# Block order made at eviction, and a new table of delays for the order of TensorE's work, in a two-layer hybrid trunk step

## The chip, the core and the metric

The kernel runs on one core of a Trainium2 chip. The core has TensorE (PE: matmuls, with its weight loads shown as PEld), VectorE (DVE), ScalarE (ACT), GpSimd (POOL) and SyncE (SP, which here only issues DMAs). Each engine executes its own instructions in the order in which they stand in the program, and waits on semaphores where it needs another engine's or a DMA's result. The metric is the device time of one execution in microseconds (us), lower is better.

## The reference, cut to what matters

```python
def mixer_inputs(x, cond, norm_g, w_ada, b_ada, w_in):
    mod = jax.nn.silu(cond) @ w_ada + b_ada
    shift, scale, gate = jnp.split(mod, 3, axis=-1)
    h = rms_norm(x, norm_g) * (1 + scale) + shift
    return jnp.split(h @ w_in, IN_OFFSETS, axis=-1), gate
...
# per layer, on 1024 latent tokens (a grid of 16 rows x 64 columns) and 256 context tokens:
qa = rope_2d(rms_norm(aq, a_qn))                 # branch A: windowed attention
ya = window_attention(qa, ka, va, ka_c, va_c, a_sink) * jax.nn.silu(ag)
qb = rms_norm(bq, b_qn)                          # branch B: 2-D neighbourhood attention
yb = neighbourhood_attention(qb, kb, vb, kb_c, vb_c, b_rpb) * jax.nn.silu(bg)
xc = depthwise_conv(cx, conv_w, conv_b)          # branch C: gated linear recurrence (LRU)
a, u = rglru_coeffs(xc, wa, ba, wx, bx, lam)
yc = (hf + hb) * jax.nn.silu(cg)
z = sigmoid(ga)*(ya @ w_br[0]) + sigmoid(gb)*(yb @ w_br[1]) + sigmoid(gc)*(yc @ w_br[2])
x = x + gate * (z @ w_out)
```

Context tokens go through the same weights. Two layers are computed (`DEPTH` = 2).

## The kernel before, in words

**Numbers and jobs.** Activations lie in SBUF with channels on the 128 partitions and tokens along the free dimension. Every fp32 operand of a large product is split in two parts, a rounded one (`_h`, made by ACT) and the remainder (`_l`, made by DVE or POOL), and a product of one 128-row piece is three matmuls: h·h, h·l, l·h. A *job* (`job`) computes 128 output columns of a projection for three chunks of tokens, `CHUNKS`: two of 512 latent tokens and one of 256 context tokens. One latent chunk of an input projection is 8 pieces x 3 = 24 matmuls with 512 moving columns. Jobs are named by what they make: `k`, `q`, `v` (attention inputs), `gt` (merge gates), `sg` (the SiLU gates of the branches), `cx` (input of the recurrence), `br` (branch outputs), `po` (output projection).

**Raster and block order.** Branch B's attention works on blocks of 16 grid rows x 8 grid columns = 128 tokens, while tokens lie in raster order (64 columns per row). Before the change the jobs of branch B (k, q, v and sg of branch B, `perm`) read the moving operand already permuted, from `Hidden.cols`: the access pattern `"p (r a c) -> p a r c"` takes runs of 8 neighbouring columns, then jumps 64. What they write is then in block order.

**The order on TensorE.** Its order is fixed by hand: a planner (`Weave`) runs while the program is built. It keeps a planned clock `W.now`, which each `mm` and `transpose` advances by a fixed cost. Chains (the recurrence `lru`, the attention `chain`, the conditioning `ada_chain`) give way with a planned time at which they may go on, and until then the planner puts pieces of jobs on TensorE: first those in `W.need`, then those in `W.spare`. The delays come from the table `T`, in planned ns: `cv` (convolution of the recurrence to its first gate product), `kc` (load of cached keys to their transposes), `ac` (conditioning product to its transposition), `nx` (last output job to the norm of the next layer), `tb` (transposed probabilities to the values product), `soft`, `pace` and others for the attention. The order on the other engines and on SP's queue is left to the framework's scheduler, so it shifts with the planned order.

**Stages.** Per layer: the recurrence with `gt` jobs between its parts (`lg` are its gate products; `xc` the convolved input, split in `xh` and `xl`; `lR`, `lS`, `lJ` its elementwise tiles); then attention, B's four head pairs first, then A's, with projections and gates between (`sc`, `sl` scores, `pt` transposed probabilities, `PT` their two parts, `o` values product, `rt` row scales); then the merge, whose last addition into `acc` stands on POOL at L1196; then the output projection and the norm for the next layer (`nps`).

## Time and profile before

| | |
|---|---|
| time, median of 3 runs (lowest to highest) | 3274.76 us (3273.53 to 3278.29) |
| the profiled execution's own time | 3279.48 us |
| its span, first to last instruction | 3277.7 us |
| busy TensorE / VectorE / ScalarE / GpSimd | 96% / 54% / 51% / 30% |
| mean granted clock of TensorE | 0.986 of full |
| DMA queue of SP, share of the 16 DMA engines | 42.9% |

The busy time of TensorE is not its work at full speed: matmuls overlap in its pipeline, and a matmul that runs at half clock is busy for longer. So its speed is read from the distance between the starts of neighbouring matmuls, and its losses from stretches in which it stands idle or has a low granted clock. A time of a run and the span of the profile differ by what lies before the first and behind the last instruction.

### The profile page before, as it was taken

Reading aid. Unit: us, or ns where it says so; the run is one execution under the profiler, and the core shown is the slowest. Engines: PE = TensorE matmul, PEld = TensorE weight load, DVE = VectorE, ACT = ScalarE, POOL = GpSimd, SP = SyncE. Lnnn points to the kernel's source line nnn. Section 1 sums busy time; section 2 is a strip of 40 time slices with the busy share of each in tenths; the row PEclk is TensorE's granted clock in tenths of the full one; section 3 lists DMA queues with packets and bytes.
Section 4 is the critical chain, followed back from the end, with each engine's and each line's share of the span. In section 5 each row is a group of like instructions: output and inputs, shape, how many; then the busy total and the mean of one; then the engine's idle time right before and its main releaser. Section 6 shows DMA issues by size and latency. Waiting matters only on the chain.

```text
span 3277.7 us, 47968 instructions
## 1 busy us (share of the span) xinstructions
PE 3149.0 (96%) x17419; PEld 2652.8 (81%) x17419; DVE 1761.3 (54%) x3255; ACT 1679.3 (51%) x3570; POOL 973.8 (30%) x827
## 2 busy tenths in 40 slices
PE   8888899999999999999999899999999999999999
PEld 5666788888888888888778787888888888888887
DVE  5564346665765664444463443566656666645531
ACT  5556345555555655433245563555555555544422
POOL 3544322222420221236433233122222221112643
PEclk9999999999999999999999999999999999999999
DMA  8556455445542332654442326354455332337543
GB/s 281 145 136 137 124 154 144 113 141 154 154 127 73 99 94 71 215 187 138 128 126 90 71 62 165 107 153 136 121 152 158 100 100 80 90 102 244 186 145 103
DMA packets 414121, 435.02 MB, mean 133 GB/s; under 512 B 43872, under 2 KB 329148, under 8 KB 412604
## 3 DMA queue, kind: packets, MB, share of 16 engines
q1 hardware_dynamic: 407900, 414.91, 42.9%
q0 software_dynamic: 5664, 16.83, 1.7%
q8 instruction: 137, 2.24, 0.3%
q14 instruction: 100, 0.82, 0.1%
q10 hardware_dynamic: 320, 0.21, 0.0%
HBM read 298.12 MB, written 137.29 MB: 133 GB/s over the span
## 4 chain that ended last, share of the span: by engine, by line
PE 73%; DVE 10%; DMA 5%; ACT 5%; issue 3%; POOL 3%; SPq 1%; ACTq 0%; DVEq 0%; POOLq 0%
PE gt L217 14%; PE sg L217 10%; PE o L217 6%; PE br L217 6%; PE pt L224 5%; PE q L217 5%; PE po L217 5%; PE v L217 4%; PE k L217 4%; PE sc L217 3%; PE sl L217 3%; POOL acc L1196 1%; PE cx L217 1%; DMA out_dram<-lR 1%; DVE lR L684 1%
## 5 line engine op out<-in xcount | busy, mean ns | idle before, releaser
L426 ACT CAST PT<-pt 128x512 fp32r<-128x512 f32 (+2 forms) x528 | 269.6, 536 | 338.6 <-PE pt L224 336.2
L427 DVE TENSOR_TENSOR PT<-pt,PT 128x512 fp32r<-128x512 f32 (+2 forms) x528 | 319.8, 621 | 93.7 <-ACT PT L426 92.5
L950 DVE TENSOR_REDUCE st<-sc 128x1 f32<-128x512 f32 x256 | 176.3, 689 | 287.9 <-PE sc L217 287.3
L217 PE MATMUL gt<-hhl,wgt_h 128*128 128x512 f32 x736 | 302.1, 410 | 2.2 <-ACT wgt_h L421 2.2
L217 PE MATMUL gt<-hhl,wgt_l 128*128 128x512 f32 x736 | 292.7, 398 | 6.6 <-POOL wgt_l L422 6.6
L217 PE MATMUL gt<-hll,wgt_h 128*128 128x512 f32 x736 | 291.4, 396 | 0.0
L422 POOL TENSOR_TENSOR wgt_l<-wgt_r,wgt_h 128x512 fp32r<-128x512 f32 x110 | 165.7, 1512 | 352.0 <-ACT wgt_h L421 325.9
L224 PE MATMUL pt<-cst,P 128*128 128x128 f32 x1856 | 269.8, 273 | 0.1
L217 PE MATMUL po<-z,wpo_h 128*128 128x512 f32 (+1 forms) x768 | 210.3, 362 | 10.7 <-ACT z L426 9.3
L224 PEld LDWEIGHTS pt<-cst,P 128*128 128x128 f32 x1856 | 217.3, 141 | 3.7 <-PE pt L224 0.5
L217 PE MATMUL br<-yl,wbr_h 128*128 128x512 f32 (+1 forms) x576 | 204.5, 355 | 3.6 <-DVE yl L427 3.6
L967 ACT ACTIVATE P<-sc,st 128x512 f32<-128x512 f32 x256 | 175.1, 684 | 59.4 <-DVE st L961 58.9
L217 PE MATMUL br<-yh,wbr_h 128*128 128x512 f32 (+1 forms) x576 | 203.7, 354 | 1.1 <-DVE gl L1195 0.8
L217 PE MATMUL br<-yh,wbr_l 128*128 128x512 f32 (+1 forms) x576 | 204.2, 355 | 0.0
L217 PE MATMUL sc<-Kpast,Q 128*128 128x512 f32 x512 | 169.7, 413 | 14.0 <-ACT P L967 14.0
L422 POOL TENSOR_TENSOR wsg_l<-wsg_r,wsg_h 128x512 fp32r<-128x512 f32 x48 | 65.7, 1378 | 380.0 <-ACT wsg_h L421 369.2
L217 PE MATMUL o<-PT,Vpast 128*128 128x256 f32 x1024 | 177.2, 295 | 0.0
L969 ACT ACTIVATE P<-sl,st 128x384 f32<-128x384 f32 (+1 forms) x320 | 170.5, 533 | 5.0 <-DVE st L957 4.8
L217 PEld LDWEIGHTS gt<-hhl,wgt_l 128*128 128x128 f32 x736 | 140.5, 191 | 39.7 <-POOL wgt_l L422 7.9
L217 PEld LDWEIGHTS po<-z,wpo_h 128*128 128x128 f32 x768 | 137.6, 193 | 33.2 <-ACT z L426 10.2
L217 PEld LDWEIGHTS gt<-hhl,wgt_h 128*128 128x128 f32 x736 | 140.8, 191 | 26.7 <-ACT wgt_h L421 2.6
L217 PE MATMUL sg<-hhl,wsg_h 128*128 128x512 f32 x384 | 161.4, 420 | 0.0
(343 smaller groups left out, 8567.8 us busy)
## 6 DMA issues: line engine op xcount, KB each, us to landing
Q<-q_d SPq DMA_DIRECT2D x160, 256.0 KB
gl<-g_d SPq DMA_DIRECT2D x48, 640.0 KB
wgt_r<-in_w_in_dram SPq DMA_DIRECT2D x110, 256.0 KB
g_d<-tgt SPq DMA_DIRECT2D x92, 256.0 KB
wa<-in_w_ada_dram POOLq DMA_DIRECT2D x64, 256.0 KB, 4.3
q_d<-q_st SPq DMA_DIRECT2D x64, 256.0 KB
wpo_r<-in_w_out_dram SPq DMA_DIRECT2D x64, 256.0 KB
yg<-y_d SPq DMA_DIRECT2D x24, 640.0 KB
```

What stands on the lines that cost most here:

```text
L217: nc.tensor.matmul(out, a, b, start=start, stop=stop)
L224: nc.tensor.transpose(out, x, idn)
L422: nc.gpsimd.tensor_sub(lo, r, f32(hi))
L426: nc.scalar.copy(hi, x)
L427: nc.vector.tensor_sub(lo, x, f32(hi))
L684: nc.vector.tensor_tensor_scan(h, a, u, st if c0 < NLAT else 0.0, ALU.mult, ALU.add)
L950: nc.vector.tensor_reduce(cm, psc, AX.X, ALU.min)
L967: nc.scalar.activation(pt[:, nl * P:(nl + 4) * P], psc, AF.Exp, bias=m, scale=-1.0, accum_out=sums[:, t, x, 1:2])
L969: nc.scalar.activation(pt[:, :nl * P], loc, AF.Exp, bias=m, scale=-1.0, accum_out=sums[:, t, x, 0:1])
L1196: nc.gpsimd.tensor_add(z, z, g)
```

## The change

All projections now read raster order. Where branch B needs block order, the operation that takes the result out of PSUM reads it with the block pattern (`blocked`) and writes it in order. A chunk of 512 tokens is 8 grid rows, so it holds half of every block; keys stay in this half-block order and the score matmul reads two runs of 64 columns per block; queries and values are put in place by their DMAs to DRAM, which become two for each one. A first group of branch B now waits for both latent chunks of its queries. The SiLU gate of branch B is in raster order and is multiplied through a pattern; its factor 0.5 moves into the row scales. The last two additions of the merge in each layer move from POOL to DVE. The planner's cost of an fp32r matmul of 512 columns goes from 216 to 228 planned ns, and nearly all delays of `T` grow, some a little (`tb` 2000 to 2200), four of them much (`cv` 9500 to 16000, `kc` 3000 to 7000, `ac` 3500 to 7000, `nx` 3500 to 8000).

```diff
-T = dict(f1=9, f2=2, kc=3000, c0=10000, cq=1, gx=3, nx=3500, yo=1500, yi=1000, aq=9000, ac=3500, ms=1800, v=3000, tok=8260, scale=1000, t0=3100, tb=2000, o=2000, soft=7000, pace=9000, lg=300, lr=8000, cv=9500, le=4000)
+T = dict(f1=9, f2=2, kc=7000, c0=10000, cq=1, gx=3, nx=8000, yo=1500, yi=1000, aq=9000, ac=7000, ms=2000, v=3200, tok=8600, scale=1100, t0=3400, tb=2200, o=2200, soft=7600, pace=9400, lg=320, lr=8500, cv=16000, le=4200)
...
-        W.now += max(n, 256) / 2.4 * (4 if a.dtype == F32 else 1) + 3
+        W.now += n / 0.6 + 3 if a.dtype == F32 else max(n * 17 / 38.4, 109) + 1
...
+    def blocked(t):
+        return t.rearrange("p (r a c) -> p a r c", r=8, a=8)
+
+    def in_blocks(t):
+        return t.rearrange("p (a r c) -> p a r c", a=8, r=8)
...
-        def cols(self, ci, perm=False):
-            c0, N = CHUNKS[ci]
-            if not perm or c0 >= NLAT:
-                return [self.at(k, ci) for k in range(KD)]
-            a0 = c0 // P
-
-            def v(t):
-                return t.rearrange("p (r a c) -> p a r c", r=ROWS, a=8)[:, a0:a0 + 4]
-            return [(v(a), v(b)) for a, b in self.lat]
+        def cols(self, ci):
+            return [self.at(k, ci) for k in range(KD)]
...
-            nc.scalar.activation(sq[:, :N], ps, AF.Square)
-            nc.vector.tensor_scalar(raw[:, :N], ps, gain, None, ALU.mult)
+            src, to = (blocked(ps), in_blocks) if blocks else (ps, lambda t: t)
+            nc.scalar.activation(to(sq[:, :N]), src, AF.Square)
+            nc.vector.tensor_scalar(to(raw[:, :N]), src, gain, None, ALU.mult)
...
-                nc.scalar.copy(vr[:, :N], ps)
+                lat = perm and c0 < NLAT
+                nc.scalar.copy(in_blocks(vr) if lat else vr[:, :N], blocked(ps) if lat else ps)
...
-                    dma(v_d[l][br][p][:, c0 // P:c0 // P + nb], f32(st[:, :nb]))
+                    if lat:
+
+                        for h in range(2):
+                            dma(v_d[l][br][p][ci * HD:(ci + 1) * HD, h:8:2], f32(st[h * HD:(h + 1) * HD]))
...
                 def put(h, part):
-                    dma(q_d[l][br][p][:, h, :, c0:c0 + N], part)
+                    if perm and c0 < NLAT:
+                        for i in range(2):
+                            dma(q_d[l][br][p][:, h, i, 0:NLAT].rearrange("d (a i k) -> d a i k", i=2, k=HD)[:, :, ci],
+                                part[:, i].rearrange("d (a k) -> d a k", k=HD))
...
             def staged(g):
+                if g.br and not g.prompt:
+                    return W.when(("Q", 1, l, g.p, 0), ("Q", 1, l, g.p, 1))
...
+                elif br:
+                    kl = g.keys.K["lat"][:, kv].rearrange("p (i a k) -> p a i k", i=2, a=8)[:, kb[0]:kb[0] + nl]
...
-                nc.vector.tensor_copy(rb, tot.unsqueeze(2).to_broadcast([P, 4, HD]))
+                nc.vector.tensor_scalar(rb, tot.unsqueeze(2).to_broadcast([P, 4, HD]), 0.5 if br else 1.0, None, ALU.mult)
...
-                nc.vector.scalar_tensor_tensor(y, y, 0.5, g, ALU.mult, ALU.mult)
+                if b == 1:
+
+                    nc.vector.tensor_tensor(in_cols(y), in_cols(y), of_rows(g), ALU.mult)
+                    nc.vector.tensor_tensor(y[:, NLAT:], y[:, NLAT:], g[:, NLAT:], ALU.mult)
+                else:
+                    nc.vector.scalar_tensor_tensor(y, y, 0.5, g, ALU.mult, ALU.mult)
...
-                    nc.gpsimd.tensor_add(z, z, g)
+                    (nc.vector if b == 0 and k >= KD - 2 else nc.gpsimd).tensor_add(z, z, g)
```

How the new table moves instructions is seen at three places.

The first is VectorE in the recurrence of the second layer, between feature block 1 and block 2. `lS`, `lR` (the scans) and the addition at the end belong to block 1; `xc` and `xl` are the convolution that block 2's first gate products need. Before:

```order
L678 TENSOR_TENSOR lS_1_1_17485<-lS_1_1_17485,lJ_1_1_17425 128x1280
L684 SCALAR_TENSOR_TENSOR lR_1_1_17423<-lA_1_1_17483,colT_1471,lS_1_1_17485 128x1024
L684 SCALAR_TENSOR_TENSOR lR_1_1_17423<-lA_1_1_17483,lS_1_1_17485 128x256
L687 TENSOR_TENSOR lR_1_0_17422<-lR_1_0_17422,lR_1_1_17423 128x1280
L614 TENSOR_SCALAR xc_2_17743<-cx_2_17632,colT_1471 128x1283
L616 SCALAR_TENSOR_TENSOR xc_2_17743<-cx_2_17632,colT_1471,xc_2_17743 128x1283 x3
```

After:

```order
L614 TENSOR_SCALAR xc_2_17771<-cx_2_17630,colT_1469 128x1283
L684 SCALAR_TENSOR_TENSOR lR_1_0_17502<-lA_1_0_17561,colT_1469,lS_1_0_17563 128x1024
L616 SCALAR_TENSOR_TENSOR xc_2_17771<-cx_2_17630,colT_1469,xc_2_17771 128x1283
L684 SCALAR_TENSOR_TENSOR lR_1_0_17502<-lA_1_0_17561,lS_1_0_17563 128x256
L616 SCALAR_TENSOR_TENSOR xc_2_17771<-cx_2_17630,colT_1469,xc_2_17771 128x1283
L678 TENSOR_TENSOR lS_1_1_17569<-lS_1_1_17569,lJ_1_1_17505 128x1280
L616 SCALAR_TENSOR_TENSOR xc_2_17771<-cx_2_17630,colT_1469,xc_2_17771 128x1283
L684 SCALAR_TENSOR_TENSOR lR_1_1_17503<-lA_1_1_17567,colT_1469,lS_1_1_17569 128x1024
L684 SCALAR_TENSOR_TENSOR lR_1_1_17503<-lA_1_1_17567,lS_1_1_17569 128x256
L427 TENSOR_TENSOR xl_2_17777<-xc_2_17771,xh_2_17776 128x1283
L687 TENSOR_TENSOR lR_1_0_17502<-lR_1_0_17502,lR_1_1_17503 128x1280
```

The convolution stood behind the scans and behind the addition of L687; it now stands between the scans, and the addition behind all of it.

The second is SP's queue at the same place. `out_dram<-lR` stores one column of a scan's result, `y_d<-lR` the sum of L687, and `wl` are the weights of block 2's gates. Before:

```order
L686 DMA out_dram<-lR_1_0_17422 128x1
L686 DMA out_dram<-lR_1_1_17423 128x1
L688 DMA y_d_2_1_109<-lR_1_0_17422 128x1280
L605 DMA wl_2_17733<-in_lru_wa_dram 64x2x64 x2
L605 DMA wl_2_17733<-in_lru_wx_dram 64x2x64 x2
L413 DMA wcx_3_r_17899<-in_w_in_dram 128x4x128
```

After:

```order
L605 DMA wl_2_17761<-in_lru_wa_dram 64x2x64 x2
L605 DMA wl_2_17761<-in_lru_wx_dram 64x2x64 x2
L413 DMA wcx_3_r_17876<-in_w_in_dram 128x4x128
L686 DMA out_dram<-lR_1_0_17502 128x1
L698 DMA g_d_0_7_143<-tgt_0_70_0_17817 128x512
L413 DMA wcx_3_r_17882<-in_w_in_dram 128x4x128
L686 DMA out_dram<-lR_1_1_17503 128x1
```

The weight loads stood behind the stores of the block before them and now stand ahead of these.

The third is TensorE at the end of the second layer's attention, in the last group of branch A (`3_6`). Before:

```order
L224 MATMUL pt_3_6_0_3_28661<-cst,P_3_6_0_28398 128x128
L224 MATMUL pt_3_6_0_3_28661<-cst,P_3_6_1_28443 128x128
L217 MATMUL sg_0_00_1_28637<-hhl_2_15374,wsg_0_00_0_h 128x512
L217 MATMUL sg_0_00_1_28637<-hll_2_15375,wsg_0_00_0_h 128x512
L217 MATMUL sg_0_00_1_28637<-hhl_2_15374,wsg_0_00_0_l 128x512
L217 MATMUL sg_0_00_1_28637<-hhl_3_15376,wsg_0_00_0_h 128x512
L217 MATMUL sg_0_00_1_28637<-hll_3_15377,wsg_0_00_0_h 128x512
L217 MATMUL sg_0_00_1_28637<-hhl_3_15376,wsg_0_00_0_l 128x512
L217 MATMUL sg_0_00_1_28637<-hhl_4_15378,wsg_0_00_4_h 128x512
L217 MATMUL sg_0_00_1_28637<-hll_4_15379,wsg_0_00_4_h 128x512
L217 MATMUL sg_0_00_1_28637<-hhl_4_15378,wsg_0_00_4_l 128x512
L217 MATMUL o_3_6_28644<-PT_3_6_0_2_28654,Vlat_0_24311 128x256 x4
```

After:

```order
L217 MATMUL o_3_6_28745<-PT_3_6_0_1_28734,Vpast_0_24441 128x256 x4
L224 MATMUL pt_3_6_0_3_28762<-cst,P_3_6_0_28509 128x128
L224 MATMUL pt_3_6_0_3_28762<-cst,P_3_6_1_28554 128x128
L217 MATMUL o_3_6_28745<-PT_3_6_0_2_28755,Vlat_0_24437 128x256 x4
L217 MATMUL o_3_6_28745<-PT_3_6_0_3_28765,Vlat_0_24437 128x256 x2
L224 MATMUL pt_3_6_1_0_28774<-cst,P_3_6_2_28605 128x128
```

Gate products stood between the transposes of a bank and the values product that needs it; in the last group of this layer no such products are left, and the `pt` and `o` rows follow each other directly up to its end.

## Rows read from the trace of the kernel before

**Rows 1.** The page: busy us, share of the span, instructions of each engine.

```profile
PE 3149.0 (96%) x17419; PEld 2652.8 (81%) x17419; DVE 1761.3 (54%) x3255; ACT 1679.3 (51%) x3570; POOL 973.8 (30%) x827
```

**Rows 2.** Timeline of TensorE, two jobs behind attention: start, length, instruction.

```profile
1333.70 0.42 PE L217 MATMUL sg<-hhl,wsg_h 128*128 128x512 f32 x1
...
1340.00 0.29 PE L217 MATMUL sg<-hhc,wsg_h 128*128 128x256 f32 x1
...
1342.88 0.40 PE L217 MATMUL sg<-hhl,wsg_h 128*128 128x512 f32 x1
...
1348.35 0.39 PE L217 MATMUL sg<-hhl,wsg_h 128*128 128x512 f32 x1
```

**Rows 3.** TensorE's waits: line waited for: us in total, times, longest.

```profile
PE lg L217 <- ACT xh L426: 14.5, 5, 4.0
...
PE lg L217 <- DVE xl L427: 8.7, 6, 2.4
...
PE adat L359 <- DVE m L353: 6.0, 1, 6.0
PE nps L217 <- DVE nacc L543: 5.7, 2, 4.2
...
PE kct L224 <- DMA kc<-in_cache_kb_dram: 4.3, 2, 3.5
```

**Rows 4.** TensorE, first recurrence: stretch, its us, busy (instructions), clock, DMA share, GB/s.

```profile
176.00:192.00 16.00, 13.75 (x62) 0.89 0.61 125
...
340.00:353.00 13.00, 6.98 (x25) 0.74 0.18 19
sum 83.00, PE 58.63; mean PE 9.77
```

**Rows 5.** The same view, three stretches of the second layer's recurrence.

```profile
1814.00:1826.00 12.00, 7.89 (x39) 0.86 0.29 93
...
1926.00:1938.00 12.00, 8.59 (x37) 0.72 0.27 88
sum 37.00, PE 24.44; mean PE 8.15
```

**Rows 6.** The same view, around the norm (two) and the cached keys (one).

```profile
1645.00:1653.00 8.00, 5.19 (x22) 1.00 0.40 114
1694.00:1706.00 12.00, 7.49 (x30) 0.86 0.29 87
...
1986.00:1996.00 10.00, 6.48 (x23) 0.83 0.45 147
```

**Rows 7.** Timelines of VectorE and ScalarE before 1818; in brackets the idle time before.

```profile
1807.48 1.49 DVE L687 TENSOR_TENSOR lR<-lR,lR 128x1280 f32<-128x1280 f32 x1 [4.37 <-DMA out_dram<-lR]
...
1818.09 1.50 DVE L427 TENSOR_TENSOR xl<-xc,xh 128x1283 fp32r<-128x1283 f32 x1 [3.34 <-ACT xh L426]
...
1815.80 0.62 ACT L609 CAST gh<-wl 128x512 fp32r<-128x512 f32 x1 [11.61 <-DMA wl<-in_lru_wx_dram]
```

**Rows 8.** Groups by line, POOL in the merge: busy, mean ns.

```profile
L1196 POOL TENSOR_TENSOR acc<-acc,gl 128x512 f32<-128x512 f32 (+1 forms) x96 | 113.0, 1199 | 68.1 <-DVE gl L1195 68.1
```

**Rows 9.** Groups by form, ScalarE 1340 to 1570: contiguous 1280 and 8-column runs of 1024.

```profile
L426 ACT CAST yh<-yg 128x1280 fp32r<-128x1280 f32 x8 | 10.0, 1264 | 7.3 <-DVE yg L1161 7.3
...
L426 ACT CAST yh<-yg 128x1024 fp32r<-128x1024 f32 x4 | 4.2, 1052 | 4.8 <-DVE yg L1161 3.0 <-PE br L217 1.8
```

**Rows 10.** One query tile: ns min/median/max; L722 takes it out of PSUM.

```profile
L722 ACT ACTIVATE q_sq<-q x48: 363/597/622, 405.0 to 2783.2; 128x512 f32<-128x512 f32 x32, 128x256 f32<-128x256 f32 x16
```

**Rows 11.** Timeline: one bank of transposed probabilities through ScalarE and VectorE.

```profile
602.23 0.60 PE L224 MATMUL pt<-cst,P 128*128 128x128 f32 x4
...
602.99 0.57 ACT L426 CAST PT<-pt 128x512 fp32r<-128x512 f32 x1
...
603.59 0.69 DVE L427 TENSOR_TENSOR PT<-pt,PT 128x512 fp32r<-128x512 f32 x1 [1.11 <-ACT PT L426]
```

**Rows 12.** Windows, branch B's attention: PE, PEld, DVE, ACT, POOL busy; clock; DMA.

```profile
590.00:660.00 70.00, 69.03 (x398) 57.65 (x397) 47.37 (x102) 41.92 (x106) 17.32 (x18) 1.00 0.38 105
```

More of the change, by code (lines that the diff above doesn't have):

```diff
@@ L220, in mm @@
             n *= d
-        W.now += max(n, 256) / 2.4 * (4 if a.dtype == F32 else 1) + 3
+        W.now += n / 0.6 + 3 if a.dtype == F32 else max(n * 17 / 38.4, 109) + 1
     def transpose(out, x, idn):
         nc.tensor.transpose(out, x, idn)
-        W.now += 110
+        W.now += 109
     def always():
@@ L699, in gate_evac, with gate_job @@
         return evac
-    def gate_job(l, H, c0w, dst, name, perm=False, chunks=(0, 1, 2)):
-        return job(I["w_in"][l], c0w, chunks, lambda ci: H.cols(ci, perm), gate_evac(dst, name), name)
+    def gate_job(l, H, c0w, dst, name, chunks=(0, 1, 2)):
+        return job(I["w_in"][l], c0w, chunks, lambda ci: H.cols(ci), gate_evac(dst, name), name)
     def gate_jobs(l, H):
@@ L708, in gate_jobs @@
         out += [((lambda chunks=(0, 1, 2), b=b, f=f, o=o: gate_job(l, H, o + f * P, s_d[l][b][f],
-                                                                   f"sg{l}_{b}_{f}{chunks[0]}", b == 1, chunks)))
+                                                                   f"sg{l}_{b}_{f}{chunks[0]}", chunks)))
                 for b, o in ((2, O_CG), (1, O_BG), (0, O_AG)) for f in range(4)]
@@ L716, in attention, with qk_norm @@
         loaded = []
-        def qk_norm(ps, N, gain, rope_c0, name, then):
+        def qk_norm(ps, N, gain, rope_c0, name, then, blocks=False):
             raw = ap.tile([P, 512], F32, tag="qraw", name=f"{name}_raw", bufs=2)
             sq = ap.tile([P, 512], F32, tag="qsq", name=f"{name}_sq", bufs=2)
-            nc.scalar.activation(sq[:, :N], ps, AF.Square)
-            nc.vector.tensor_scalar(raw[:, :N], ps, gain, None, ALU.mult)
+            src, to = (blocked(ps), in_blocks) if blocks else (ps, lambda t: t)
+            nc.scalar.activation(to(sq[:, :N]), src, AF.Square)
+            nc.vector.tensor_scalar(to(raw[:, :N]), src, gain, None, ALU.mult)
             def finish():
@@ L801, in evac @@
                 qk_norm(ps, N, dcol[l][:, 2 * br + 1:2 * br + 2], c0 if rope and c0 < NLAT else None,
-                        f"k{name}_{ci}", then)
-            W.need.append((cond, job(w_in, c0w, (0, 1, 2), lambda ci: H.cols(ci, perm), evac, f"k{name}", start)))
+                        f"k{name}_{ci}", then, perm and c0 < NLAT)
+            W.need.append((cond, job(w_in, c0w, (0, 1, 2), lambda ci: H.cols(ci), evac, f"k{name}", start)))
         def v_jobs(br, p, cond):
@@ L831, in evac @@
                 W.later(T["v"], finish)
-            W.need.append((cond, job(w_in, c0w, (0, 1, 2), lambda ci: H.cols(ci, perm), evac, f"v{name}")))
+            W.need.append((cond, job(w_in, c0w, (0, 1, 2), lambda ci: H.cols(ci), evac, f"v{name}")))
         def q_jobs(br, p, cond):
@@ L842, in put @@
                 def put(h, part):
-                    dma(q_d[l][br][p][:, h, :, c0:c0 + N], part)
+                    if perm and c0 < NLAT:
+                        for i in range(2):
+                            dma(q_d[l][br][p][:, h, i, 0:NLAT].rearrange("d (a i k) -> d a i k", i=2, k=HD)[:, :, ci],
+                                part[:, i].rearrange("d (a k) -> d a k", k=HD))
+                    else:
+                        dma(q_d[l][br][p][:, h, :, c0:c0 + N], part)
                 def then(qn):
@@ L848, in evac @@
                 qk_norm(ps, N, dcol[l][:, 2 * br:2 * br + 1], c0 if rope and c0 < NLAT else None,
-                        f"q{name}_{ci}", then)
-            W.need.append((cond, job(w_in, c0w, (0, 1, 2), lambda ci: H.cols(ci, perm), evac, f"q{name}")))
+                        f"q{name}_{ci}", then, perm and c0 < NLAT)
+            W.need.append((cond, job(w_in, c0w, (0, 1, 2), lambda ci: H.cols(ci), evac, f"q{name}")))
         class Keys:
@@ L952, in score @@
                 loc = psl[:, :nl * P]
-                kl = g.keys.K["ctx"][:, kv] if g.prompt else g.keys.K["lat"][:, kv, kb[0] * P:(kb[0] + nl) * P]
+                if g.prompt:
+                    kl = g.keys.K["ctx"][:, kv]
+                elif br:
+                    kl = g.keys.K["lat"][:, kv].rearrange("p (i a k) -> p a i k", i=2, a=8)[:, kb[0]:kb[0] + nl]
+                else:
+                    kl = g.keys.K["lat"][:, kv, kb[0] * P:(kb[0] + nl) * P]
                 mm(loc, qh, kl, True, False)
@@ L1149, in merge_jobs, with of_rows, in_cols @@
         Y, Z, acc, gated, gate = {}, [], [], {}, {}
+        def of_rows(x):
+            return x[:, 0:NLAT].rearrange("p (r a c) -> p a r c", r=ROWS, a=8)
+        def in_cols(x):
+            return x[:, 0:NLAT].rearrange("p (a r c) -> p a r c", a=8, r=ROWS)
         def gate_y(b, f):
@@ L1160, in run @@
                 nc.vector.scalar_tensor_tensor(g, t, 1.0, g, ALU.add, ALU.mult)
-                nc.vector.scalar_tensor_tensor(y, y, 0.5, g, ALU.mult, ALU.mult)
+                if b == 1:
+                    nc.vector.tensor_tensor(in_cols(y), in_cols(y), of_rows(g), ALU.mult)
+                    nc.vector.tensor_tensor(y[:, NLAT:], y[:, NLAT:], g[:, NLAT:], ALU.mult)
+                else:
+                    nc.vector.scalar_tensor_tensor(y, y, 0.5, g, ALU.mult, ALU.mult)
                 gated[b, f] = y
@@ L1170, in run @@
                 if b == 1:
[L1171 to L1173 removed]
+                    split(of_rows(yh), of_rows(yl), in_cols(y))
                     split(yh[:, NLAT:], yl[:, NLAT:], y[:, NLAT:])
```

4 lines of the change are left out of this document (1 added, 3 removed).

## The prediction

> **What bounds the kernel now.** I read the page first: TensorE is busy for 3149 of 3277.7 us, the others for little more than half [rows 1]. So time goes away only where TensorE's own instructions get shorter, or where it stops standing idle or running at its low clock. The timeline of TensorE shows the first kind. Behind the first layer's attention two gate jobs of the same shape follow each other, with no chain between them: a chunk of branch B, which reads runs of 8 columns, and one of branch A, which reads 512 neighbours. From start to start the 24 matmuls of the first take 1340.00 - 1333.70 = 6.30 us, 262 ns each, those of the second 1348.35 - 1342.88 = 5.47 us, 228 ns each [rows 2]. The list of TensorE's waits names the second kind: the gate products of the recurrence wait for the convolution's two parts, the transposition of the conditioning for a copy, the norm for its sum of squares, the cached keys' transposes for their load [rows 3]. [...] In attention, more than half of the time, TensorE hardly waits: 69.0 of 70 us busy at full clock [rows 12].
>
> **The change part by part.** The sum is made against the profiled execution's 3279.48 us; the median is 3274.76, and I take the sum off that.
>
> *Contiguous reads.* Branch B's k, q, v and sg jobs are four kinds x 4 head pairs x 2 latent chunks x 24 matmuls x 2 layers = 1536 matmuls. At 262.5 - 227.9 = 34.6 ns each [rows 2] they give 53 us. The score products of branch B take a new pattern, runs of 64 columns; per column this has an eighth of the jumps of the old one, so at most 34.6 x 6 / 64 = 3 ns each on 256 matmuls, under 1 us: nothing.
> The row says that short runs cost. [...]
>
> *Block order at eviction.* Eight-column runs now stand in 32 Squares on ACT, 32 multiplications on DVE and 16 copies on ACT. The trace has no such read from PSUM. The nearest row is a ScalarE cast with the same runs in SBUF: 1052 ns for 1024 columns, against 1264 for 1280 contiguous ones, so nothing but the length [rows 9]. I take 0; the other end is in the rivals. The cover is the gap between a chunk's last matmul and the product that needs its square (`ms`, 2.0 planned us, against 0.60 us for the Square [rows 10]). The extra DMA issues (two instead of one per part of q and per v) are 48 more on SP's queue, off the path. Rescaling and the gate's two multiplications replace operations of the same size.
>
> *Delays of the recurrence (`cv`).* I take a stretch's loss as its idle time plus the lost share of the clock. For six stretches of the first layer's recurrence, of which the first and the last are shown: 83.0 - 58.6 = 24.4 us idle, and clock losses that add up to 14.3 (the two shown: 0.11 x 16 = 1.8 and 0.26 x 13 = 3.4) [rows 4]: 38 us in all. For three of the second layer: 37.0 - 24.4 = 12.6 idle and 8.4 of clock (1.7 and 3.4 in the two shown) [rows 5]: 21 us. Their waits are for `xh` and `xl`, 14.5 + 8.7 us, and for the conditioning (`ac`), 6.0 [rows 3].
> Why they end is seen in the order. Before, in the second layer, VectorE reached `xc` only behind the addition of L687, which waited 4.4 us for the store of a scan's column; and ScalarE stood 11.6 us until the weights `wl` had landed, which SP issued behind those stores; `xl` was ready at 1819.6 [rows 7]. Now `xc` stands between the scans and the weight loads ahead of the stores, while TensorE has more gate products between `cx` and the first `lg`. What is late next is only the scans' own sum, for which nobody on TensorE waits in this stage. I take 30 of the 38 us (one stretch, 318 to 328, waits for a PSUM bank, which `cv` does not change) and 18 of the 21.
>
> *Norm and cached keys (`nx`, `kc`).* Around the norm 2.8 + 4.5 idle and 0.14 x 12 = 1.7 of clock are lost: 9 us; at the cached keys 3.5 + 1.7 = 5 [rows 6]. With the products put later and other jobs in front, I take 7 and 4.
>
> *Last additions of the merge.* An addition costs POOL 1.2 us [rows 8], and VectorE some 0.69 for this size [rows 11]; the output projection waits for the last one, once a layer: 2 us in all. Other work on POOL's queue at that place (weight remainders) becomes earlier.
>
> *What the change adds.* At the end of the second layer's attention the gate jobs are used up: transposes and values products stand directly behind each other. From the first transpose of a bank to its remainder part the trace has 603.59 + 0.69 - 602.23 = 2.05 us [rows 11]. Counted through with two banks in flight, seven banks take 10.5 us, where some 52 matmuls of half or a quarter of the columns need about 6: 4.5 us of waits, and with a fall of the clock 6. Before, gate products covered this.
> In branch B's attention TensorE's work gets shorter by 53 us over some 800, VectorE's and ScalarE's does not: VectorE goes from 47.4 of 70 us [rows 12] to about 0.72. Their queues get longer at each hand-over; I take 5 us for both layers, between 0 and the 40 of the rival below. The next pair's keys have the same distance in products as before, less 0.5 us; nothing.
>
> **Sum:** 53 + 30 + 18 + 7 + 4 + 2 - 6 - 5 = 103 us, so 3274.8 - 103 = **3172 us** (3176 for an execution like the profiled one).
>
> **The rivals.**
> *All waits go and nothing new comes:* 53 + 38 + 21 + 9 + 5 + 2 = 128, **3147 us**. For it: the new distances exceed the old ones by more than the waits. Against it: the used-up gate jobs stand in the order. 0.13.
> *Attention gives the reads back:* VectorE and ScalarE set the pace in branch B, and of the 53 us three quarters (k, q, v) are lost again: 3172 + 40 = **3212 us**. For it: hand-overs of about 2 us for each bank. Against it: neither engine is over 0.72 there. 0.12.
> *The waits only move:* the recurrence is bound by VectorE's and ScalarE's own work, which the delays don't shorten, so only the reads count: 53 - 11 = 42, **3233 us**. For it: from one block to the next the products on TensorE got no more. Against it: the 4.4 and 11.6 us above are waits for stores and loads, not work [rows 7]. 0.11.
> *Short runs are free on TensorE*, the 34.6 ns having another cause: 3172 + 53 = **3225 us**. The two jobs of [rows 2] differ in nothing else that I see. 0.02. [...]
> *Slower: the read of PSUM in runs of 8 is slow.* Every latent chunk of B's k, q, v, 48 in all, then keeps its PSUM bank and the `ms` product back. To end above 3274.8 each must cost 103 / 48 = 2.1 us on TensorE beyond the 1.4 us of slack (2.0 less 0.60), so an eviction of 4.1 us, seven times what the row has [rows 10]. At that point it decides; at eight times, **3303 us**. 0.04.
>
> **How the numbers follow.** The forecast has 0.56; its own range, from the bounds of 30, 18, 7 and the 5 of attention, is 3152 to 3192. Some 0.02 is left for what I did not think of. The range 3144 to 3218 takes in the forecast, the better case and attention's pace, and leaves out 0.19. A measurement of this kernel tells about 0.2%, 6.5 us, from no change. Everything but the last rival is faster by more: faster 0.94, the same 0.02, slower 0.04.
>
> **What would show it.** Right: gate jobs of branch B at 228 ns per matmul; 1819-like waits for `xh` and `xl` gone from the list, with the clock at 1.00 in both recurrences; `nps` and `kct` gone; a new short wait of `o` for `PT` at the end of the second layer's attention. Wrong: Squares of k and q above 0.6 us; waits of `ms`, `sc` or `o` in branch B that add up to tens of us; `lg` still waiting, then for VectorE's scans; or branch B's chunks still at 6.3 us.

## The result, and the profile after

| | before | changed |
|---|---|---|
| median, beside each other on one chip | 3276.53 us | 3245.15 us |
| profiled execution, its span | 3277.7 us | 3249.5 us |
| mean granted clock of TensorE | 0.986 | 0.977 |

The ratio is 0.9904, 95% interval 0.9882 to 0.9926: 31 us less. The forecast was 103 us less (3172 us, range 3144 to 3218). So it is faster, but by a third of the forecast, and outside the range. The median of the kernel before itself differs from one occasion to the next by up to 0.5% (below), so what follows compares runs made beside each other, or ratios to the kernel before that was run beside them. The profile of the changed kernel is of the slowest of its four executions (3251.3 us).

The page of the changed kernel, beside [rows 1]:

```profile
PE 3101.2 (95%) x17419; PEld 2651.7 (82%) x17419; DVE 1787.8 (55%) x3275; ACT 1701.3 (52%) x3586; POOL 974.8 (30%) x815
```

TensorE is busy for 48 us less; the span became only 28 us shorter, so 20 us of idle time were added. The timeline of TensorE, a k job of branch B in the second layer, first matmul of one chunk and of the next:

```profile
1958.41 0.40 PE L217 MATMUL k<-hhl,wk_h 128*128 128x512 f32 x1
...
1963.91 0.39 PE L217 MATMUL k<-hhl,wk_h 128*128 128x512 f32 x1
```

24 matmuls in 5.50 us are 229 ns each, as in the contiguous job of [rows 2]. Taking them out of PSUM in runs of 8 cost nothing here, a median of 598 ns against 597: the tile `q_sq`, in the form of [rows 10] (the multiplication on VectorE, `q_raw`, has a median of 740 ns, against 741 before):

```profile
L723 ACT ACTIVATE q_sq<-q x48: 363/598/616, 405.8 to 2749.0; 128x512 f32<-128x512 f32 x32, 128x256 f32<-128x256 f32 x16
```

The list of TensorE's waits, as in [rows 3] (line waited for: us in total, times, longest):

```profile
PE sc L217 <- ACT P L986: 28.4, 12, 3.7
PE lg L217 <- ACT lR L641: 17.0, 2, 14.2
PE k L217 <- ACT wk_h L421: 10.9, 1, 10.9
...
PE kct L224 <- DMA kc<-in_cache_kb_dram: 9.0, 1, 9.0
PE lg L217 <- DVE xl L427: 8.0, 3, 3.5
...
PE po L217 <- ACT z L426: 5.1, 2, 2.6
...
PE pt L224 <- DVE Y L1054: 3.8, 2, 1.9
...
PE nps L217 <- DVE nacc L543: 1.5, 1, 1.5
```

The waits for `xh` and for VectorE's copy `m` of the conditioning are gone as forecast, and `nps` is short. The waits for `xl` are not gone: 8.0 us, against 8.7. And four others are longer: for a gate tile `lR`, for weights `wk_h`, for the cached keys, and for ScalarE's exponentials `P`, twice the sum of before, which was:

```profile
PE sc L217 <- ACT P L967: 14.0, 21, 1.2
```

Two of these places by their windows (the columns of [rows 12]), first before, then in the changed kernel:

```profile
240.00:256.00 16.00, 14.85 (x76) 11.15 (x74) 0.69 (x1) 7.64 (x11) 2.43 (x2) 0.91 0.94 143
362.00:384.00 22.00, 19.27 (x86) 15.27 (x84) 0.00 (x0) 3.76 (x8) 6.89 (x7) 0.92 0.57 172
```

```profile
240.00:256.00 16.00, 1.85 (x11) 1.42 (x10) 1.73 (x2) 1.18 (x3) 0.48 (x1) 0.70 0.98 134
362.00:384.00 22.00, 9.18 (x41) 7.32 (x40) 1.31 (x1) 2.19 (x4) 6.39 (x6) 0.66 0.57 181
```

TensorE works for 1.9 of 16 and 9.2 of 22 us, where it worked for 14.9 and 19.3 before, and the mean granted clock is 0.70 and 0.66 instead of 0.91 and 0.92.

**Where the loss stands, stage by stage.** This table is worked out from the traces: for each stage, the distance between its first matmul and that of the next stage, less what the stage's matmuls take at their undisturbed pitch (227 ns for 512 contiguous columns, 267 in runs of 8, which is the median over all such jobs; 176, 118 and 109 for 384, 256 and 128 columns and less; 454 for four of the conditioning's, which run side by side: their starts lie 5 to 8 ns apart). What is left is idle time and low clock, in us. The granted clock in the records of the kernel before is 1.00 or 0.50; from 349.4 to 351.9, at 0.50, matmuls of 512 contiguous columns start 0.43 us apart and last 0.63 us, and from 352.3 to 356, at 1.00, 0.23 and 0.39. "Attention A" begins with branch A's first k job, while the last head pair of B is still running. "condition" is the kernel before with the new wait of branch B's first group alone (run 18), "table" with the new table alone (run 2), "reads" the changed kernel with the old table (run 17), "changed" the changed kernel in run 12; "shifted" (run 8) and "three" (run 14) come below.

```
                        before condition     table     reads   changed   shifted     three
start                     38.6      38.9      37.0      37.6      36.9      36.9      38.9
recurrence 1              62.0      61.7      66.3      61.0      60.0      59.0      54.3
first keys 1               5.8       5.4       7.0       8.5       7.9       8.5       4.4
attention B 1             12.0      12.8      12.8      18.6      19.4      19.4      18.2
attention A 1             27.9      32.9      20.3      35.8      41.7      28.2      28.5
merge, output, norm       25.4      23.1      18.3      13.8      13.8      14.1      14.6
recurrence 2              23.7      22.3      18.8      23.2      15.6      14.3      13.9
first keys 2               7.0       5.7      10.4       9.3      11.6      12.3      12.9
attention B 2             11.4      13.1      12.6      18.2      18.0      19.2      18.0
attention A 2             27.1      34.6      21.1      34.1      39.8      31.3      30.9
merge, output, end        11.5      12.7      13.2      11.8      11.9       7.9      11.2
all losses               252.3     263.2     237.7     272.0     276.7     251.0     245.9
work at full pitch      3019.9    3019.9    3019.9    2958.4    2958.4    2958.4    2958.4
```

Where one kernel was profiled twice (runs 1 and 17, 5 and 18, the result and run 12), a single row differs by up to 5 us, so only larger differences, or those that all such runs show, say something.

The first recurrence, which was to give 30 us, lost 60.0 us, against 62.0. Branch A's attention, of which the forecast expected 6 us at its end, lost 27 us more in both layers, and B's 14 us.

### The profile page after: what moved, and what is told of

Same layout as the page of the kernel before. It is cut to its first block, busy times and chain, and to the rows that moved or that the text cites. A ratio compares the mean times of both kernels' runs of the same rounds, so it can differ in the third digit from the quotient of the medians.

```text
span 3249.5 us, 48117 instructions
## 1 busy us (share of the span) xinstructions
PE 3101.2 (95%) x17419; PEld 2651.7 (82%) x17419; DVE 1787.8 (55%) x3275; ACT 1701.3 (52%) x3586; POOL 974.8 (30%) x815
## 4 chain that ended last, share of the span: by engine, by line
PE 71%; DVE 9%; ACT 6%; DMA 6%; issue 4%; POOL 3%; SPq 0%; ACTq 0%; DVEq 0%; POOLq 0%
PE gt L217 14%; PE sg L217 10%; PE po L217 7%; PE o L217 6%; PE pt L224 5%; PE q L217 5%; PE k L217 4%; PE v L217 4%; PE sc L217 3%; PE br L217 3%; PE sl L217 3%; PE cx L217 2%; POOL acc L1224 2%; DVE lR L684 1%; DMA out_dram<-lR 1%
## 5 line engine op out<-in xcount | busy, mean ns | idle before, releaser
L422 POOL TENSOR_TENSOR wgt_l<-wgt_r,wgt_h 128x512 fp32r<-128x512 f32 x110 | 177.4, 1620 | 346.0 <-ACT wgt_h L421 314.4
L986 ACT ACTIVATE P<-sc,st 128x512 f32<-128x512 f32 x256 | 175.4, 685 | 57.9 <-DVE st L980 57.4
L217 PE MATMUL sc<-Kpast,Q 128*128 128x512 f32 x512 | 168.7, 411 | 28.4 <-ACT P L986 28.4
L217 PEld LDWEIGHTS gt<-hll,wgt_h 128*128 128x128 f32 x736 | 141.6, 192 | 24.9 <-issue 0.5
```

What stands on the lines that cost most here:

```text
L217: nc.tensor.matmul(out, a, b, start=start, stop=stop)
L422: nc.gpsimd.tensor_sub(lo, r, f32(hi))
L986: nc.scalar.activation(pt[:, nl * P:(nl + 4) * P], psc, AF.Exp, bias=m, scale=-1.0, accum_out=sums[:, t, x, 1:2])
```

## The experiments

**1 and 2: the change cut in two.** Reads: the changed kernel with the old `T` and the old costs. Table: the kernel before with the new ones.

```diff
-T = dict(... kc=7000, ... nx=8000, ... ac=7000, ... cv=16000, le=4200)
+T = dict(... kc=3000, ... nx=3500, ... ac=3500, ... cv=9500, le=4000)
-        W.now += n / 0.6 + 3 if a.dtype == F32 else max(n * 17 / 38.4, 109) + 1
+        W.now += max(n, 256) / 2.4 * (4 if a.dtype == F32 else 1) + 3
```

> The changed kernel with the old table of delays and the old planned costs of matmuls: contiguous reads, order at eviction and the two moved additions alone. Theory 1 (the reads give their 53 us, and the new plan then loses some 25 us in new stalls): 3276 - 53 - 2 = about 3220 us, faster than the changed kernel. Rival (branch B's attention gives the reads back whatever the plan is, 'attention gives the reads back' of the prediction): 3276 - 13 - 2 = about 3260 us, slower than the changed kernel, with waits of q_ms, sc and o in branch B that add up to 40 us.

> The kernel before with the new table of delays and the new planned costs, reads still in runs of 8 columns. Theory 1 (the plan loses): 3276 + 25 = about 3300 us, slower than before. Rival (the plan gains the 48 us of the recurrence as predicted, and what was lost is in the attention's reads): about 3230 us.

Reads alone: 3238.83 us, 0.9879 (0.9863 to 0.9896), faster than the whole change by the ratios. The table alone: 3258.66 us, 0.9942 (0.9924 to 0.9961). So neither theory stands. Apart, the parts gain some 40 and 19 us; together they gain 31: what the table gains in the old order it does not gain in the new one.

**3 and 4: groups of delays back.** The changed kernel with the recurrence's entries old, then with the attention's.

```diff
-... ac=7000, ... lg=320, lr=8500, cv=16000, le=4200
+... ac=3500, ... lg=300, lr=8000, cv=9500, le=4000
```

```diff
-ms=2000, v=3200, tok=8600, scale=1100, t0=3400, tb=2200, o=2200, soft=7600, pace=9400
+ms=1800, v=3000, tok=8260, scale=1000, t0=3100, tb=2000, o=2000, soft=7000, pace=9000
```

> The changed kernel with only the recurrence's delays set back (cv 16000 to 9500, ac 7000 to 3500, lr, le, lg by some per cent). Theory 1 (the first layer's recurrence gained nothing by them, the second some 12 us, and the 14.4 us wait for the weights wcx is new): within 8 us of the changed kernel's 3245. Rival (the prediction: the delays are worth 48 us): 3293 us.

> The changed kernel with only the attention's delays set back (ms, v, tok, scale, t0, tb, o, soft, pace). Theory 1 (the six waits of 3.7 us of branch A's scores for ScalarE's exponentials, each with a fall of the clock, come from these entries, and so do the 5 us at the end of the second layer's attention): 3245 - 25 = 3220 us, and the six waits are gone. Rival (they come from VectorE's and ScalarE's work and stay wherever the products are put): 3245 us, the six waits still there.

3233.94 us, 0.9862 (0.9833 to 0.9891): not slower but some 14 us faster by the ratios, so the 48 us of the forecast are not in these delays. 3241.98 us, 0.9889 (0.9873 to 0.9905): of the 25 us that theory 1 gave, some 5 came. `sc` waited for 31.7 us, 27 times; the waits had only spread.

**5: the new condition alone.** `staged` in the kernel before.

```diff
             def staged(g):
+                if g.br and not g.prompt:
+                    return W.when(("Q", 1, l, g.p, 0), ("Q", 1, l, g.p, 1))
                 return W.when(("Q", g.br, l, g.p, 2 if g.prompt else g.t0 // 4))
```

> The kernel before, with one condition of the change alone: the first group of branch B waits for both latent chunks of its queries. Table, costs and strided reads are the old ones, and no instruction is added. In the order TensorE's rows of branch A's attention then stand as in the reads-only kernel. Theory 2 (the condition shifts the groups of attention against the projection jobs, so that the norm of the third query chunk meets the scores sc00_x_4_1 on VectorE): waits of about 2.5 us before sc00_x_4_1, three times a layer, branch A's attention loses some 15 us more in all, and the kernel is slower than before: about 3290 us. Rival (the waits come with the faster reads, not with the order): branch A as before, 3278 us.

3283.72 us, 1.0046 (1.0030 to 1.0062): slower, by 15 us. The later start of branch B's first group shifts all groups of attention against the projection jobs, also in branch A, which has no such condition. By the table branch A's attention loses 12.5 us more by it (run 18), all stages together 10.9. TensorE's waits for `P` in this kernel, beside 14.0, 21 times, before:

```profile
PE sc L217 <- ACT P L969: 23.1, 14, 2.3
```

What happens there is seen best in the changed kernel, where it is worst. Timelines of VectorE, ScalarE and TensorE before the scores `sc00_0_4_1`:

```profile
955.61 1.65 DVE L741 SCALAR_TENSOR_TENSOR q_raw<-q_sq,q_raw 128x512 f32<-128x512 f32 x1
...
960.15 0.99 DVE L738 TENSOR_TENSOR q_raw<-q_raw,q_sq 128x256 f32<-128x256 f32 x1
961.06 0.61 DVE L980 CUSTOM_DVE_ANT_0 sl<-sl,mask,st 128x384 f32<-128x384 f32 x1
...
961.62 0.93 DVE L740 TENSOR_TENSOR q_sq<-q_me,q_sq 128x256 f32<-128x256 f32 x1
962.47 0.56 DVE L983 TENSOR_TENSOR st<-st,sink 128x1 f32<-128x1 f32 x1
```

```profile
963.06 0.29 ACT L984 ACTIVATE st<-sink,st 128x1 f32<-128x1 f32 x1 [1.47 <-DVE st L983]
963.26 0.67 ACT L986 ACTIVATE P<-sc,st 128x512 f32<-128x512 f32 x1
```

```profile
964.08 1.22 PE L217 MATMUL sc<-Kpast,Q 128*128 128x512 f32 x2 [3.60 <-ACT P L986]
```

`sc` has two PSUM banks, which it shares with `sl`; the next one is free only after the exponential of L986, which needs the row minimum of L980 and L983. On VectorE the norm of two query chunks (L738 to L741) now stands ahead of these and between them. It meets the same group in three of the four head pairs, in both layers: six waits of 3.6 to 3.7 us, 21.9 of the 28.4 us. The mean clock in the 20 us around each is 0.83, around one 0.91. In run 5 the same six places wait 2.3 us each.

**8: the groups shifted back.** The changed kernel, branch A's first group later; no work is added.

```diff
+                if g.t0 == 0 and g.p == 0 and not g.br:
+                    yield W.now + 9000
                 if g.t0 == 0:
                     W.mark(("start", g.br, l, g.p))
```

> The changed kernel; the first group of branch A's attention is put 9000 planned ns later, with other jobs in front. No work is added. In the order the norms of the second and third query chunk then stand in the context group (`_8`), ahead of the scores sc00_x_4. Theory 2 (phase of groups and query jobs): the six waits of 3.7 us before sc00_x_4_1 are gone or under 1 us, with the clock's falls behind them some 25 us less: 3220 us. Rival (ScalarE and VectorE fall behind wherever the norms stand): the waits move to other scores and add up to the same: 3245 us.

3216.98 us, 0.9843 (0.9826 to 0.9860): 20 us below the changed kernel by the ratios, and branch A's attention loses 22 us less by the table. The six waits are 0.9 to 1.0 us each. This is the first large part of what was missing. The waits of this kernel, then one stretch (the columns of [rows 12]), first in the changed kernel and then in this one:

```profile
PE sc L217 <- ACT P L986: 12.1, 12, 1.7
```

```profile
956.00:976.00 20.00, 16.39 (x71) 13.53 (x70) 12.29 (x25) 7.86 (x23) 7.67 (x8) 0.83 0.47 134
```

```profile
956.00:976.00 20.00, 19.05 (x108) 16.28 (x108) 11.60 (x30) 10.47 (x29) 8.37 (x9) 1.00 0.57 160
```

**6: the state column copied.** Why are `wk` and `kc` late? SP's queue in the changed kernel (`y_d<-lR` stores the sum of L687):

```profile
363.34 0.32 SPq L688 DMA_DIRECT2D y_d<-lR  x1
363.71 5.95 SPq L1355 DMA_DIRECT2D bias_d<-t_d  x8
...
371.23 0.93 SPq L413 DMA_DIRECT2D wk_r<-in_w_in_dram  x2
```

The sum writes over the tile whose column is being stored, so it waits 9.3 us for that store:

```profile
361.82 1.49 DVE L687 TENSOR_TENSOR lR<-lR,lR 128x1280 f32<-128x1280 f32 x1 [9.28 <-DMA out_dram<-lR]
```

The experiment stores a copy:

```diff
+                last = rp.tile([P, 1], F32, tag="last", name=f"last{l}_{f}_{d}", bufs=4)
+                nc.vector.tensor_copy(last, R[d][:, e:e + 1])
-                dma(O[6][...], R[d][:, e:e + 1])
+                dma(O[6][...], last)
```

> The changed kernel; the state's last column is copied to a tile of its own (16 copies of 128 x 1 on VectorE), and the store of the column reads the copy, so that the sum of L687 no longer waits for the store. Theory 3 (the sum's wait of 9.3 us for the store holds back the store of the sum in SP's queue, and behind it the weights wk and the cached keys kc): the waits of k for wk_h (10.9) and of kct for kc (9.0) shrink to less than half, with their falls of the clock some 20 us less: 3225 us. Rival (the weights are late because of the bias tables' copies in SP's queue and of the DMA engines): 3245 us, waits of 8 us and more stay.

3231.46 us, 0.9883 (0.9868 to 0.9899), some 7 us less by the ratios, of 20; the intervals overlap a little. The two waits are not halved:

```profile
PE k L217 <- ACT wk_h L421: 8.6, 1, 8.6
...
PE kct L224 <- DMA kc<-in_cache_kb_dram: 7.5, 1, 7.5
```

Run 12, the changed kernel again, has 10.3 and 6.8 us there, so only the first may be shorter. SP's queue of this kernel:

```profile
347.54 0.33 SPq L690 DMA_DIRECT2D y_d<-lR  x1
...
349.34 11.04 SPq L1357 DMA_DIRECT2D bias_d<-t_d  x9
...
361.98 0.93 SPq L413 DMA_DIRECT2D wk_r<-in_w_in_dram  x2
```

The sum's store goes 16 us earlier, the weights only 9: nine copies of the bias tables are next in the queue. And TensorE comes to the k job 6.6 us earlier too, so the wait is hardly shorter.

**7: `cv` alone back** (16000 to 9500).

> The changed kernel with only cv set back, 16000 to 9500. Theory 4 (the long delay cv brings the first layer's 14.4 us wait behind the late weights wcx): that wait is gone, and all of the 11 us that the old recurrence delays gave together are there: 3234 us. Rival a (the conditioning's delay ac, with its loads of wa, brings it): the wait stays, 3245 us. Rival b (the prediction: cv is worth 48 us in both layers): above 3280 us.

3239.31 us, 0.9911 (0.9895 to 0.9928): the same as the changed kernel. The wait behind `wcx` is gone as theory 4 says, but its 11 us are not gained: `lg` waits for `xh` again, 25.8 us, and `k` for `wk_h` 14.4. So the long `cv` does end the waits for `xh`, and others take their place.

**9 to 12: the bias copies closer together, and repairs together.**

```diff
-                W.later(100000 + 100000 * l + 3000 * r, lambda l=l, r=r: rows(l, r))
+                W.later(100000 + 1500 * (16 * l + r), lambda l=l, r=r: rows(l, r))
```

> The changed kernel; the 32 copies of the bias tables (L1355) are spread 1500 planned ns apart instead of 3000 with a gap between the layers, so that none is left for the end of the first recurrence, where before nine of them stood in SP's queue ahead of the weights wk. In the order the weights now stand ahead of the last recurrence's stores too. Theory 3b (what holds the weights wk is SP's queue, with these copies as its last part): the wait of k for wk_h (10.9) is gone, and with the fall of the clock some 15 us: 3230 us. Rival (the weights are late because the DMA engines are full, or TensorE waits there for the next thing): the wait becomes another of the same size, 3245 us.

> The changed kernel with three edits of the runs before together: shifted first group of branch A, copied state column, early bias tables. Theory (the three repair different places, so they add up: about 28 by the groups, 7 to 15 by the column, 15 by the bias tables): 3245 - 50 = about 3195 us. Rival (the first recurrence is bound by its own chain, so the waits there only move again): 3245 - 28 - 5 = about 3212 us, as the shifted groups alone.

> The run with three edits, with the recurrence's delays set back as well (cv, ac, lr, le, lg). Theory (the long cv costs the wait for wcx in the first layer and gains in the second): within 6 us of the run with three edits, the first layer faster, the second slower. Rival (with the queue repaired the long cv gives what the prediction expected of it): slower than the run with three edits by 20 us or more.

> The changed kernel itself, unedited, beside the three others on the same chip, so that differences between them don't rest on different runs of the kernel before. Ratio to before 0.990, 3245 us; the waits before sc00_x_4_1, of lg behind wcx, of k for wk_h and of kct for kc are there as in its first profile.

Bias early 3247.39 us, 0.9921 (0.9906 to 0.9935); three edits 3216.18, 0.9830 (0.9813 to 0.9848); with the old delays 3216.36, 0.9831; the changed kernel again 3239.28, 0.9904 (0.9891 to 0.9917). In run 9 the wait for `wk_h` is gone, and nothing is won. A wait of 13.8 us stands at a gate job for its weights, and ScalarE's timeline says why:

```profile
PE gt L217 <- ACT wgt_h L421: 16.5, 3, 13.8
```

```profile
288.21 1.26 ACT L426 CAST xh<-xc 128x1283 fp32r<-128x1283 f32 x1 [1.48 <-DVE xc L616]
289.38 1.13 ACT L421 CAST wgt_h<-wgt_r 128x512 fp32r<-128x512 f32 x2
```

ScalarE was busy, nearly without a gap, from 260.9 to 286.7 with the recurrence's own chain, and the weights' cast stood behind it. Seven table loads of 1.28 us each (`ACT_TABLE_LOAD`), 9.0 us, are part of this chain; no experiment takes them out. The rival of run 9 is right, and that of run 10: the waits move. Run 11 came out within 6 us, as its theory said, but for another reason: by the traces the old delays of the recurrence changed neither layer's sum of recurrence and first keys by more than 2 us.

**13 to 15: half of the bias copies out of the first recurrence.**

```diff
+        late_rows.extend(lambda r=r: rows(1, r) for r in range(ROWS))
...
             with pool(f"att{l}", side=there) as ap:
+                for r, fn in enumerate(late_rows):
+                    W.later(60000 + 20000 * r, fn)
+                late_rows.clear()
```

> The changed kernel; the 16 copies of the bias tables for the second layer are made from the first layer's attention on, where planned delays put them, and not at the end of the first recurrence; in SP's queue ten of them now stand behind the weights wk, and the others are spread out. Theory 3c (the copies as such hold SP's queue and the DMA engines in the first recurrence, so moving them inside it only moves the wait, and taking half of them out of it ends one): the wait of k for wk_h is under 3 us, no new wait of its size stands in the first recurrence, 3243 - 15 = about 3228 us. Rival (the first recurrence is bound by its own chain of products, exponentials and scans, so its waits add up to the same whatever SP does): 3240 us or more.

> The three edits together, with the second layer's bias copies later in place of closer together. Theory 3c: some 15 to 20 us below the run with three edits, so about 3198 us. Rival (the recurrence's own chain): the same as the run with three edits, 3216 us.

> The same with the recurrence's delays (cv, ac, lr, le, lg) set back. Theory (the long delays gain 10 us in the second layer's recurrence, and with SP's queue free nothing is lost for them in the first): 8 us or more slower than the run before it. Rival (the long delays only move the waits in both recurrences): within 5 us of it, or faster.

3243.68 us, 0.9872 (0.9859 to 0.9886); **3209.95 us, 0.9766 (0.9752 to 0.9779)**; 3219.21 us, 0.9794 (0.9781 to 0.9808). In runs 13 and 14 the wait for `wk_h` is gone and none takes its place; that of `lg` for `lR` stays in run 13, 16.2 us. What half the copies are worth is not settled. By the ratios it is some 10 us alone (run 13 against 12) and 21 beside the other repairs (0.9830 to 0.9766, run 14 against 10). But the kernel before was 13 us slower beside runs 13 to 15 than beside runs 9 to 12; by the medians run 13 is 4 us slower than run 12, and run 14 only 6 us faster than run 10. By the stages, the first recurrence and its first keys lose 62.3 us in run 13 and 58.7 in run 14, against 67.9 in the changed kernel. So SP's queue holds a part of some 6 to 9 us, little more than the spread of the table. I take the rest for the recurrence's own chain; no run shows that. With the queue repaired, the long delays gain 9 us (run 14 against 15, beside each other), as that theory had it. Run 14 is the fastest of all, 75 us below the kernel before.

**16 to 18: two sizes beside each other.** The reads-only kernel with branch A's groups shifted (10000 in the diff of run 8), that kernel unshifted, and the condition alone.

> The reads-only kernel (old table, old planned costs) with branch A's first group put 10000 planned ns later, so that the norms of the query chunks stand ahead of the scores sc00_x_4, as in the run with shifted groups. Theory 2 (the phase is all that the condition costs): the waits of 2.5 us are gone, 15 us or more less than the reads-only kernel beside it, ratio to before about 0.983; and since the shifted groups with the new table gave 0.984, the new table is worth nothing once the phase is right. Rival (the new table's delays are worth their waits in the second layer, some 10 us): 0.987 or more.

> The reads-only kernel again, beside the one with shifted groups and the one with the condition alone on the same chip: ratio to before 0.988.

> The kernel before with the condition alone again. Its distance to the reads-only kernel on the same chip is what contiguous reads, eviction in blocks and the two moved additions are worth in the same order: 50 us by the prediction's terms (53 + 2 - 5), 45 by the earlier medians, 55 by the earlier ratios.

0.9874 (0.9855 to 0.9892), 0.9872 (0.9854 to 0.9890) and 1.0039 (1.0025 to 1.0053), medians 3238.23, 3237.81 and 3291.36. Between the last two lie 53.6 us: that is what reads, eviction and moved additions give in an unchanged order. The shift gains nothing with the old table; with the new one it gave 20 us. `sc` still waits in run 16:

```profile
PE sc L217 <- ACT P L986: 20.7, 18, 2.0
```

The six waits became shorter only from 2.3 to 1.6 us, where run 8 has 0.9. So the rival's 0.987 was measured, but the run does not decide theory 2: it did not remove the waits that it was to remove. What run 8 shows is the place of the loss.

## Why the prediction was wrong

By its own steps, from runs beside each other where that can be:

- *Contiguous reads, 53 us, merge additions 2, branch B's hand-overs -5*: together 50, measured 53.6 (run 17 against 18). The mechanism is right; that the size fits so well is in part luck, as the parts are off both ways. The one job of [rows 2] had 262.5 ns per matmul, the median over all such jobs is 267, so the reads give 61.5 us at full pitch (3019.9 to 2958.4 in the table). Branch B's attention gave back 11, not 5, and the first keys another 3 to 7 (runs 5 and 1, 18 and 17). The output projection waits for `z` 5 us less (10.0 in run 18, below, and 5.1 in run 17), where 2 were expected; that the additions alone do it, and what else the stage of merge, output and norm gained, no run isolates. The rival that runs of 8 columns are free on TensorE (0.02) does not hold for this operand: 267 ns per matmul against 227.

```profile
PE po L217 <- ACT z L426: 10.0, 2, 5.0
```

- *Block order at eviction, nothing*: right, 598 ns against 597 on ScalarE, 740 against 741 on VectorE. (That rival's price at eight times comes to 3305 us, not 3303.)
- *The condition on the first group*: not priced at all. It costs 13 to 15 us (runs 5 and 18). This is the first step that failed. It stands in the change, and the forecast gave it no term.
- *Delays of the recurrence, 30 + 18 us*: the first recurrence gave nothing beyond the spread, 61.0 to 60.0 (reads against changed), the second 7.6, of which its first keys gave back 2.3. This is the step that failed most. Its argument was that the old waits were for stores and loads, not for work, so that products put later would not wait. The waits for `xh` did end, but the loads do not come earlier when the products come later, and the time went to waits for loads and for a gate tile instead. SP's issue of the second half of `wcx` and ScalarE's cast of it, before:

```profile
240.57 0.90 SPq L413 DMA_DIRECT2D wcx_r<-in_w_in_dram  x1
```

```profile
254.15 0.62 ACT L421 CAST wcx_h<-wcx_r 128x512 fp32r<-128x512 f32 x1
```

And in the changed kernel:

```profile
240.55 0.38 SPq L413 DMA_DIRECT2D wcx_r<-in_w_in_dram  x1
```

```profile
254.82 0.62 ACT L421 CAST wcx_h<-wcx_r 128x512 fp32r<-128x512 f32 x1 [16.45 <-DMA wcx_r<-in_w_in_dram]
255.35 0.68 ACT L641 ACTIVATE lR<-lg,dcol 128x512 f32<-128x512 f32 x1
```

The load is issued at the same time in both, and cast at nearly the same time (when it landed before, no row shows; at the latest at 254.15). Only ScalarE's order is new: the cast stands ahead of the eviction of `lg`, so gate products wait 14.2 us for a PSUM bank. This is the place of the forecast's rival "the waits only move" (3233 us), to which 0.11 was given. Its price is near by luck, since it holds neither the condition nor branch A's waits, and its reason, that the recurrence is bound by VectorE's and ScalarE's own work, is shown at one place alone (run 9). The clock at 1.00 in both recurrences, a sign of being right, did not come: 0.70 in 240 to 256.
- *Norm 7, cached keys 4*: `nps` waits for `nacc` 1.4 to 1.5 us in all runs with the new table, 2.9 to 5.8 with the old one, so this wait did shrink; that the stage got faster by it in the new order, the table does not show (13.8 in both), and no run sets `nx` or `kc` back alone. `kct` waited 9.0 us instead of 4.3 (6.8 in run 12), since `kc` is issued behind the sum's store and TensorE came earlier.
- *The end of the second layer's attention, -6*: right in kind; the waits of `o` there add up to 3.6 us, the longest of 2.1 for `Y` and the others for `PT`, as forecast. The granted clock stayed at 1.00 there (2885 to 2912), so the fall of the clock that this term adds to its waits did not come. The condition alone already brings 2.1 us of them (run 18). But the six waits of the scores, in both layers, were in no term, and with them branch A lost 27 us more than before: by runs 18, 17 and 12 it is 12 by the condition, 2 more with the reads and 12 more with the table, each within some 4 us.

The sum that the runs give: +13 for the condition, -54 for the reads, +10 for the table in this order (0.9872 to 0.9904; 1.5 by the medians, 4.7 by the profiles, so its size is uncertain), so -31. The mechanism of the reads was right; what failed was to take waits of an order as a stock that a longer delay uses up, and to give the new condition no price.

## What to carry to other kernels

A longer delay did not shorten a wait that ended with a load, because the load was issued no earlier: see what the issue stands behind, and move that first. Here taking half of the copies out of SP's queue, storing a copy of the column and shifting the groups brought the changed kernel from 0.9904 to 0.9766 (45 us by the ratios, 29 by the medians); with the recurrence's old delays they give 0.9794. A condition added to one group shifts every later group against the work beside it; price it by the waits behind it in all stages in which the groups then meet other jobs, not at the place where it stands. Where an order is planned by hand, cut the change into reads and order, and measure both: here each part alone was faster than the kernel before, and one of them was, by the ratios, faster than the two together.

## What was not expected of the hardware

In two windows the busy share of the 16 DMA engines said little of what they moved: 238 to 256 of the changed kernel and of the kernel with the copied column (DMA share and GB/s at the end):

```profile
238.00:256.00 18.00, 3.85 (x25) 3.26 (x23) 3.73 (x7) 1.55 (x4) 0.81 (x2) 0.73 1.01 152
```

```profile
238.00:256.00 18.00, 9.07 (x44) 7.72 (x42) 5.17 (x12) 6.57 (x12) 2.66 (x4) 0.70 0.58 169
```

The one is at 1.01 of its share with 152 GB/s, the other at 0.58 with 169, and a weight of 128 x 512, the second half of `wcx`, needs 14.3 us from issue to cast in the one, 8.6 in the other (241.21 to 249.82). What makes packets slow there is not settled.

The median of the kernel before lay between 3270.3 and 3285.5 us on the occasions when it was run, 0.5% apart, more than most differences here. On one chip it was 3272.4 us once and 3278.4 us half an hour later, so the chip is not all of it.
